# Two rings of split weight blocks as one tile each, with the stationary blocks 64 bytes in

## The chip, the cores and the metric

The kernel runs on one core of a Trainium2 chip. The metric is the device time of one execution in microseconds; the time before is the median of three executions.

## The reference

The kernel computes two layers on 256 tokens of width 1024. Each layer is a mixer (layer 0: latent attention with a low-rank query and key/value path; layer 1: attention over keys that an indexer selects), a layer norm, a PEER mixer (product keys choose 128 experts of 16,384 for each token), and a second layer norm.

```python
for i in range(DEPTH):
    if i % N_MIXERS == 0:
        m = _mla_mixer(x, ...)
    else:
        m = _dsa_mixer(x, ...)
    x = _layernorm(DN_ALPHA * x + m, ln_gain[i, 0], ln_bias[i, 0])
    f = _peer(x, peer_w_q[i], peer_sub_keys[i], peer_w_down[i], peer_w_up[i])
    x = _layernorm(DN_ALPHA * x + f, ln_gain[i, 1], ln_bias[i, 1])
...
# in _peer, for each block of tokens
u = w_down[e_blk]
a = jnp.einsum('td,ted->te', x_blk, u).astype(jnp.float32)
hg = (jax.nn.gelu(a, approximate=False) * g_blk).astype(w_up.dtype)
return jnp.einsum('te,ted->td', hg, w_up[e_blk]).astype(x_blk.dtype)
```

## The kernel before

**Split products.** Each float32 factor is split into a high part, rounded to the matmul's fp32r format, and a low part, the remainder. A product is three matmuls: high x high, high x low, low x high (`mm3`, `proj`, `rows`). The activations, transposed, live in two tiles `xh` and `xl` of 128 partitions x 8 x 256 values.

**PEER without a gather.** The kernel multiplies by all experts. In the down stage (tile `d`) each of 128 blocks of `w_down` gives the activations of 128 experts for 256 tokens; one-hot matmuls (tile `G`) place the gates, which multiply the gelu of `d`; the up stage (tile `y`) multiplies the result by 128 blocks of `w_up` into four PSUM banks. The two stages stand in each of two layers.

**The stream of weights.** `Stream` (line 51) carries every weight matrix as a row of blocks of 128 x 1024 values, in the order of the `ws.add` lines. A block is loaded by a DMA on SP's queue into one of four `raw` buffers (`_load`), cast by ScalarE into a `hi` buffer (L96), and subtracted by VectorE into a `lo` buffer (L100), or by GpSimd (L98) where `pooled` or `share` says so. `get()` hands out the next block and issues the cast and the subtraction of the block three further on (`AHEAD`), and the load of one three beyond that. `open()` and `close()` do the same in parts at the ends of the stages (`finish`), in an order written out there.

`his` and `los` are pools of four buffers of 4,096 bytes in each partition, used in turn; a buffer is overwritten when the last instruction that read it is done.

**Two uses of a block.** In `proj` and in the `up` helper of the latent attention the block is the weights: a slice of 128 columns is loaded into TensorE, and 256 columns of `xh`, `xl` (or of `V` and `U` in the groups `qn` and `qr`) stream past. So it is with mla_h (groups `h`, `krope`), mla_qk (`qn`, `qr`, `kn`), blocks 4 on of peer_q (`pq`), down (`d`), dsa_iq (`qi`), dsa_ik (`ki`, whose slices have 72 columns) and dsa_qk (`q`). In `rows` and in the lead units of `finish` the block is the moving operand, 512 columns at a time, and slices of `xh` and `xl` are the weights: mla_v and dsa_v (`v`), mla_w_o, dsa_w_o and up (`y`), blocks 0 to 3 of peer_q (`qw`).

**Where the operands stand.** In the built program `xh`, `xl`, the `raw`, `hi` and `lo` buffers and the arena begin at multiples of 512 bytes in their partitions. `V` and `U` (`oh_tile`, also used for `hot` and `gate`) lie behind the small tiles and begin at 64 bytes past a multiple of 128.

**What sets the order.** The tile framework orders the instructions of each engine by a simulated timeline at compile time, and draws the waits from the bytes that instructions touch. In the sparse attention part of the order is written out: `link` puts TensorE's matmuls and, from the first key projection on, VectorE's instructions (`dve`, which is also `ws.dve` there) in program order. In that part the steps of `attention` with `late` follow one another so: key projections of heads 4 and 5 (`meanwhile(4)`, whose two `get()` calls issue the cast and the subtraction of the last dsa_qk block and of the first dsa_w_o block), rotary copies and products of those heads (L507 to L516), scores of heads 2 and 3, their softmax (L547 to L559), then key projections of heads 6 and 7, outputs `o` of heads 0 and 1, and scores `s` of heads 4 and 5.

Of the kernel before, what the change touches and what calls it, by code (L numbers as in the profile page):

```python
# [11 lines left out]
F32R = mybir.dt.float32r  # L12
# [6 lines left out]
P = 128  # L19
T = 256  # L20
D = 1024
NC = D // P
# [21 lines left out]
FIRST = 4  # L44
WARM = 9
EARLY = 11264
GSCALE = 2.0 ** 14
DSA_POOL = 3
MAGIC = 12582912.0


class Stream:
# [5 lines left out]
    def __init__(self, nc, raw, hi, lo):  # L58
        self.nc, self.raw, self.hi, self.lo = nc, raw, hi, lo
        self.dve = self.act = lambda emit: emit()  # L60
        self.blocks, self.ready = [], []
        self.n_loaded = self.n_split = self.n_taken = 0
        self.tiles = []
        self.early = {}
        self.share = 0

    def add(self, src, w=D):
        self.blocks += [(src[i], w) for i in range(src.shape[0])]

    def _load(self, upto):  # L70
        while self.n_loaded <= min(upto, len(self.blocks) - 1):
            src, w = self.blocks[self.n_loaded]
            if self.n_loaded in self.early:
                t = self.early[self.n_loaded]
            else:
                t = self.raw.tile([P, D], F32, tag="raw", name=f"raw{self.n_loaded}")
                self.last = self.nc.sync.dma_start(t[:, :w], src).ins
            self.tiles.append(t)
            self.n_loaded += 1
# [8 lines left out]
    def _split(self, upto, pooled=False):  # L88
        nc = self.nc
        while self.n_split <= min(upto, len(self.blocks) - 1):  # L90
            w = self.blocks[self.n_split][1]
            self._load(self.n_split)
            raw = self.tiles[self.n_split][:, :w]
            hi = self.hi.tile([P, D], F32R, tag="hi", name=f"hi{self.n_split}")[:, :w]
            lo = self.lo.tile([P, D], F32R, tag="lo", name=f"lo{self.n_split}")[:, :w]
            self.act(lambda: nc.scalar.copy(hi, raw))  # L96
            if pooled or self.share and self.n_split % self.share == 0:
                nc.gpsimd.tensor_tensor(lo, raw, hi.bitcast(F32), op=ALU.subtract)  # L98
            else:
                self.dve(lambda: nc.vector.tensor_tensor(lo, raw, hi.bitcast(F32), op=ALU.subtract))  # L100
            self.ready.append((hi, lo))
            self.n_split += 1
# [7 lines left out]
    def open(self, queue):  # L110

        i = self.n_split
        assert i == self.n_taken
        self._load(i)
        raw = self.tiles[i]
        hi = self.hi.tile([P, D], F32R, tag="hi", name=f"hi{i}")
        lo = self.lo.tile([P, D], F32R, tag="lo", name=f"lo{i}")
        queue("act", lambda: self.nc.scalar.copy(hi, raw))
        self.ready.append((hi, lo))
        self.n_split += 1  # L120
        self.n_taken += 1
        return i
# [39 lines left out]
def tile_trunk(ctx: ExitStack, tc: tile.TileContext, ins, out: bass.AP):  # L162
    nc = tc.nc
    def pool(name, bufs, **kw):
        return ctx.enter_context(tc.tile_pool(name=name, bufs=bufs, **kw))
# [1 line left out]
    lead = pool("lead", 1)  # L167
    wide = pool("wide", 1)
    raws = pool("raws", 4)
    his = pool("his", 4)  # L170
    los = pool("los", 4)
    big = pool("big", 1)
    const = pool("const", 1)
    dram = pool("dram", 1, space=bass.MemoryType.DRAM)
# [35 lines left out]
    nc.vector.memset(ones, 1.0)  # L210
    nc.vector.memset(mhalf, -0.5)

    ws = Stream(nc, raws, his, los)
    ws.add(ins["mla_h"][0:6])
    ws.add(ins["mla_qk"])
    ws.add(ins["mla_v"])
    ws.add(ins["mla_w_o"])
    ws.add(ins["peer_q"][0])
    ws.add(ins["down"][0])
    ws.add(ins["up"][0])  # L220
    ws.add(ins["dsa_v"][0:FIRST])
    ws.add(ins["dsa_iq"])
    ws.add(ins["dsa_ik"], 576)
    ws.add(ins["dsa_v"][FIRST:NC])
    ws.add(ins["dsa_qk"])
    ws.add(ins["dsa_w_o"])
    ws.add(ins["peer_q"][1])
    ws.add(ins["down"][1])
    ws.add(ins["up"][1])

    chains = {}

# [574 lines left out]
    def dsa():  # L807
# [82 lines left out]
        for t in range(2):  # L890
            for n in range(2):
                nc.scalar.copy(v[:, t, n * 512 : (n + 1) * 512], v4[t][n])
        ws.share = DSA_POOL
        for h in range(0, HEADS, 2):
# [22 lines left out]
    def peer(li):  # L917
# [77 lines left out]
        def choose():  # L995
# [40 lines left out]
            gt, i1 = tail[:, 0:T], tail[:, T : 2 * T]  # L1036
            nc.vector.tensor_scalar(gt, pg[:, :T], GSCALE, None, op0=ALU.mult)
            nc.vector.tensor_copy(gate16, gt)
# [23 lines left out]
        def place(g4, done):  # L1062
# [8 lines left out]
            if done < P:  # L1071
                nc.scalar.mul(A[:, done:, tsl], pv[:, done:, :], 1.0 / GSCALE)
            if done:
                nc.vector.scalar_tensor_tensor(A[:, :done, tsl], pv[:, :done, :], 1.0 / GSCALE, A[:, :done, tsl],
                                               op0=ALU.mult, op1=ALU.mult)
# [54 lines left out]
    xt = Arena(arena, 30720).take(NC, T)  # L1130
    piece = [slice(c, c + 2) for c in range(0, NC, 2)]
    raw0 = raws.tile([P, D], F32, tag="raw", name="raw0")
    hi0 = his.tile([P, D], F32R, tag="hi", name="hi0")
    lo0 = los.tile([P, D], F32R, tag="lo", name="lo0")
    nc.sync.dma_start(raw0, ins["mla_h"][0])
    for c in range(0, NC, 4):
        last = nc.sync.dma_start(xt[:, c : c + 4, :], ins["xT"][c // 4])
    ws.blocks = ws.blocks[1:]
    with tc.issue_after(last.ins):
        ws._load(2)  # L1140

    def first(o):

# [129 lines left out]
```

## Time and profile before

| | |
|---|---|
| median of 3 executions | 1838.15 us (1837.89 to 1838.22) |
| profiled execution, span | 1836.6 us |
| TensorE busy | 1824.8 us, 99% |
| VectorE busy | 1317.8 us, 72% |
| ScalarE busy | 1056.2 us, 58% |
| GpSimd busy | 362.8 us, 20% |
| read from HBM | 329.16 MB, 182 GB/s over the span |

The profile is of one execution. A row of a timeline begins with the start and the length in microseconds, then the engine (PE is TensorE, DVE VectorE, ACT ScalarE, POOL GpSimd), the line in the kernel, the operation, and the tile written, with the tiles read behind the arrow; for a matmul the first of these is the moving operand or the weights as the program names them. "x12" is a count, and square brackets hold idle time before and what ended it. Lines L253 and L256 are helpers that issue every matmul and transpose, so groups of matmuls are told apart by their tiles. Matmuls are pipelined: each is shown longer than the distance between two starts, and the distance is what a run of them costs. A row of groups has the count, then busy time and mean ns of one, then the idle time before them.

### The profile page before, as it was taken

What the parts mean: (1) busy time and instruction counts of PE and PEld (TensorE: products, weight loads), DVE (VectorE), ACT (ScalarE), POOL (GpSimd) and SP (SyncE); (2) the same over time, 40 slices, a digit from 0 to 9 for tenths busy, and PEclk for the clock granted to TensorE, in tenths of its full rate; (3) what the DMA queues carried; (4) which work ended last, traced back from release to release, by engine and by line L of the source; (5) the groups of instructions that cost most, each with busy time, mean ns of one, the idle gap of its engine ahead of it and who ended that gap; (6) DMA issues with size and microseconds to landing.
All of it is one profiled execution on the core that took longest, in us unless ns stands there. A gap on an engine that the chain in (4) does not pass through costs nothing.

```text
span 1836.6 us, 32394 instructions
## 1 busy us (share of the span) xinstructions
PE 1824.8 (99%) x12495; PEld 1671.9 (91%) x12495; DVE 1317.8 (72%) x2348; ACT 1056.2 (58%) x1834; POOL 362.8 (20%) x265
## 2 busy tenths in 40 slices
PE   9999999999999999999999999999999999999998
PEld 8899999999998888888889899999999988888886
DVE  6689986788865555555688789957888765555555
ACT  6655456887764444444466555548877654444443
POOL 2002442445510000000022004504455300000000
PEclk9999999999999999999999999999999999999999
DMA  7554555444456555555646445554444475555553
GB/s 240 195 179 167 184 184 172 162 161 152 161 174 237 192 192 194 193 194 195 210 157 227 164 165 182 173 193 161 154 157 155 168 235 192 194 193 194 195 195 116
DMA packets 93468, 335.47 MB, mean 183 GB/s; under 512 B 10368, under 2 KB 11392, under 8 KB 93312
## 3 DMA queue, kind: packets, MB, share of 16 engines
q1 hardware_dynamic: 93024, 332.87, 52.9%
q8 instruction: 98, 1.61, 0.4%
q14 instruction: 58, 0.48, 0.1%
q10 hardware_dynamic: 288, 0.52, 0.1%
HBM read 329.16 MB, written 4.19 MB: 182 GB/s over the span
## 4 chain that ended last, share of the span: by engine, by line
PE 98%; DVE 1%; issue 1%; ACT 0%; DMA 0%; SPq 0%; DVEq 0%; POOLq 0%; POOL 0%; ACTq 0%
PE d L253 40%; PE y L253 40%; PE pq L253 4%; PE G L253 3%; PE q L253 3%; PE v L253 1%; PE qw L253 1%; PE s L253 1%; PE ps L253 1%; PE h L253 1%; PE qi L253 1%; PE o L253 1%; PE qn L253 0%; DMA arena<-in_xT 0%; PE kn L253 0%
## 5 line engine op out<-in xcount | busy, mean ns | idle before, releaser
L100 DVE TENSOR_TENSOR lo<-raw,hi 128x1024 fp32r<-128x1024 f32 (+1 forms) x579 | 763.9, 1321 | 345.0 <-ACT hi L96 344.1
L96 ACT CAST hi<-raw 128x1024 fp32r<-128x1024 f32 (+1 forms) x583 | 611.0, 1049 | 561.7 <-PE d L253 265.3
L253 PE MATMUL d<-xh,hi 128*128 128x256 f32 x2048 | 585.1, 286 | 0.0
L253 PE MATMUL d<-xh,lo 128*128 128x256 f32 x2048 | 579.2, 283 | 0.0
L253 PE MATMUL d<-xl,hi 128*128 128x256 f32 x2048 | 579.2, 283 | 0.0
L253 PEld LDWEIGHTS d<-xl,hi 128*128 128x128 f32 x2048 | 392.7, 192 | 0.0
L253 PEld LDWEIGHTS d<-xh,lo 128*128 128x128 f32 x2048 | 392.6, 192 | 0.0
L253 PEld LDWEIGHTS d<-xh,hi 128*128 128x128 f32 x2048 | 392.5, 192 | 0.0
L253 PE MATMUL y<-lo,xh 128*128 128x512 f32 x1088 | 337.7, 389 | 0.0
L253 PE MATMUL y<-hi,xh 128*128 128x512 f32 x1088 | 337.7, 390 | 0.0
L253 PE MATMUL y<-hi,xl 128*128 128x512 f32 x1088 | 337.3, 389 | 0.0
L1055 POOL TENSOR_TENSOR gate<-hot,gate 128x512 f16<-128x512 f16 x128 | 221.8, 1751 | 310.6 <-DVE hot L1053 310.6
L253 PEld LDWEIGHTS y<-lo,xh 128*128 128x128 f32 x1088 | 204.2, 188 | 42.7 <-DVE lo L100 0.3
L253 PEld LDWEIGHTS y<-hi,xl 128*128 128x128 f32 x1088 | 204.2, 188 | 42.4
L253 PEld LDWEIGHTS y<-hi,xh 128*128 128x128 f32 x1088 | 203.8, 188 | 41.8
L347 POOL TENSOR_TENSOR st<-st,mhalf 128x1 f32<-128x1 f32 x8 | 4.4, 551 | 827.2 <-DVE st L345 827.2
L1059 ACT ACTIVATE gate<-hot,rest 128x128 f16<-128x128 f16 x512 | 166.1, 413 | 0.9 <-DVE hot L1053 0.9
L1114 ACT CAST xh<-arena 128x512 fp32r<-128x512 f32 x128 | 79.8, 623 | 145.6 <-PE y L253 145.4
L1115 DVE TENSOR_TENSOR xl<-arena,xh 128x512 fp32r<-128x512 f32 x128 | 88.2, 692 | 73.5 <-ACT xh L1114 73.5
L1053 DVE TENSOR_TENSOR hot<-iota,place 128x1024 f16<-128x1024 f16 x128 | 84.9, 703 | 49.1 <-PE G L253 49.0
L1024 POOL TENSOR_TENSOR arena<-arena 128x800 f32<-128x800 f16 x32 | 78.8, 2482 | 38.8 <-DVE arena L1022 38.0
L253 PE MATMUL G<-gate,hot 128*128 128x128 f16 x1024 | 70.1, 221 | 0.0
(222 smaller groups left out, 1739.5 us busy)
## 6 DMA issues: line engine op xcount, KB each, us to landing
raw<-in_down SPq DMA_DIRECT2D x256, 512.0 KB, 3.2
raw<-in_up SPq DMA_DIRECT2D x256, 512.0 KB, 4.3
raw<-in_peer_q SPq DMA_DIRECT2D x24, 512.0 KB, 4.4
raw<-in_dsa_qk SPq DMA_DIRECT2D x16, 512.0 KB, 3.2
raw<-in_mla_w_o SPq DMA_DIRECT2D x8, 512.0 KB, 5.9
arena<-in_peer_q SPq DMA_DIRECT2D x8, 512.0 KB, 4.3
raw<-in_dsa_v SPq DMA_DIRECT2D x8, 512.0 KB, 4.3
raw<-in_dsa_w_o SPq DMA_DIRECT2D x8, 512.0 KB, 3.7
```

What stands on the lines that cost most here:

```text
L96: self.act(lambda: nc.scalar.copy(hi, raw))
L100: self.dve(lambda: nc.vector.tensor_tensor(lo, raw, hi.bitcast(F32), op=ALU.subtract))
L253: return pe(lambda: nc.tensor.matmul(o, l, r, start=start, stop=stop, skip_group_check=True))
L347: nc.gpsimd.tensor_tensor(st[:, 5:6], st[:, 4:5], mhalf, op=ALU.pow)
L1024: nc.gpsimd.tensor_tensor(o.rearrange("p k c -> p c k"), same, cell[t][:, h, :, None].to_broadcast([P, CELLS, TOPK]), op=ALU.mult)
L1053: nc.vector.tensor_tensor(hot, iota4[:, None].to_broadcast([P, 2, P, 4]), place16[:, :, None, four].to_broadcast([P, 2, P, 4]), op=ALU.is_ ...
L1055: nc.gpsimd.tensor_tensor(gate[:, 0], hot[:, 1].rearrange("p c j -> p j c"), gate16[:, four, None].to_broadcast([P, 4, P]), op=ALU.mult)
L1059: nc.scalar.mul(gate[:, 1, j, :], hot[:, 1, :, j], rest[:, t : t + 1])
L1114: nc.scalar.copy(hh, a)
L1115: nc.vector.tensor_tensor(al, a, hh.bitcast(F32), op=ALU.subtract)
```

## The change

The four `hi` buffers become one tile `hi` of 4 x 1024 + 64 values, the four `lo` buffers one tile `lo` of the same size. Block i stands at place i mod 4. A block added with `moving=True` begins at the start of its place; any other begins `SKEW` = 16 values, 64 bytes, further on, and so ends 64 bytes into the next place. The matrix peer_q is added in two parts, since its first four blocks are moving operands and the others weights. The first block, which was handled outside the stream, is now counted as block 0; `share` and the first `_load` are shifted by one to fit.

```diff
+RING = 4
+SKEW = 16
...
-    def add(self, src, w=D):
+    def add(self, src, w=D, moving=False):
         self.blocks += [(src[i], w) for i in range(src.shape[0])]
+        self.moving += [moving] * src.shape[0]
+
+    def parts(self, i):
+
+        skew = 0 if self.moving[i] else SKEW
+        at = i % RING * D + skew
+        return [ring[:, at : at + self.blocks[i][1]] for ring in (self.hi, self.lo)]
...
-            hi = self.hi.tile([P, D], F32R, tag="hi", name=f"hi{self.n_split}")[:, :w]
-            lo = self.lo.tile([P, D], F32R, tag="lo", name=f"lo{self.n_split}")[:, :w]
+            hi, lo = self.parts(self.n_split)
             self.act(lambda: nc.scalar.copy(hi, raw))
-            if pooled or self.share and self.n_split % self.share == 0:
+            if pooled or self.share and (self.n_split - 1) % self.share == 0:
...
-        hi = self.hi.tile([P, D], F32R, tag="hi", name=f"hi{i}")
-        lo = self.lo.tile([P, D], F32R, tag="lo", name=f"lo{i}")
+        hi, lo = self.parts(i)
...
-    his = pool("his", 4)
-    los = pool("los", 4)
+    rings = pool("rings", 1)
...
-    ws = Stream(nc, raws, his, los)
+    ring = [rings.tile([P, RING * D + 64], F32R, tag=k, name=k) for k in ("hi", "lo")]
+    ws = Stream(nc, raws, *ring)
     ws.add(ins["mla_h"][0:6])
     ws.add(ins["mla_qk"])
-    ws.add(ins["mla_v"])
-    ws.add(ins["mla_w_o"])
-    ws.add(ins["peer_q"][0])
+    ws.add(ins["mla_v"], moving=True)
+    ws.add(ins["mla_w_o"], moving=True)
+    ws.add(ins["peer_q"][0][0:FIRST], moving=True)
+    ws.add(ins["peer_q"][0][FIRST:])
     ws.add(ins["down"][0])
-    ws.add(ins["up"][0])
-    ws.add(ins["dsa_v"][0:FIRST])
+    ws.add(ins["up"][0], moving=True)
+    ws.add(ins["dsa_v"][0:FIRST], moving=True)
     ws.add(ins["dsa_iq"])
     ws.add(ins["dsa_ik"], 576)
-    ws.add(ins["dsa_v"][FIRST:NC])
+    ws.add(ins["dsa_v"][FIRST:NC], moving=True)
     ws.add(ins["dsa_qk"])
-    ws.add(ins["dsa_w_o"])
-    ws.add(ins["peer_q"][1])
+    ws.add(ins["dsa_w_o"], moving=True)
+    ws.add(ins["peer_q"][1][0:FIRST], moving=True)
+    ws.add(ins["peer_q"][1][FIRST:])
     ws.add(ins["down"][1])
-    ws.add(ins["up"][1])
+    ws.add(ins["up"][1], moving=True)
...
-    hi0 = his.tile([P, D], F32R, tag="hi", name="hi0")
-    lo0 = los.tile([P, D], F32R, tag="lo", name="lo0")
...
-    ws.blocks = ws.blocks[1:]
+    hi0, lo0 = ws.parts(0)
+    ws.n_loaded = ws.n_split = ws.n_taken = 1
+    ws.tiles.append(raw0)
+    ws.ready.append((hi0, lo0))
     with tc.issue_after(last.ins):
-        ws._load(2)
+        ws._load(3)
```

More of the change, by code (lines that the diff above doesn't have):

```diff
@@ L61, in __init__ @@
         self.blocks, self.ready = [], []
+        self.moving = []
         self.n_loaded = self.n_split = self.n_taken = 0
```

## The prediction

> **What bounds the kernel now.** I read the page first, then the groups kept apart by shape, the chain in order of time, and the timeline of the stretches in which the alignment of the operands differs.
>
> ```profile
> span 1836.6 us, 32394 instructions
> PE 1824.8 (99%) x12495; PEld 1671.9 (91%) x12495; DVE 1317.8 (72%) x2348; ACT 1056.2 (58%) x1834; POOL 362.8 (20%) x265
> PEclk9999999999999999999999999999999999999999
> PE d L253 40%; PE y L253 40%; PE pq L253 4%; PE G L253 3%; PE q L253 3%; PE v L253 1%; PE qw L253 1%; PE s L253 1%; PE ps L253 1%; PE h L253 1%; PE qi L253 1%; PE o L253 1%; PE qn L253 0%; DMA arena<-in_xT 0%; PE kn L253 0%
> ```
>
> TensorE is busy all the time at full granted clock, and the chain is its own queue. Only two things can move the end: how far apart matmuls start, and new waits of TensorE. The first is read from runs of matmuls in the chain (start, length, count), the counts from the groups:
>
> ```profile
> 23.22 2.88 PE krope L253 x24
> 43.13 3.83 PE kn L253 x32
> 151.56 146.63 PE d L253 x1222
> 548.60 348.19 PE y L253 x1536
> ...
> L253 PE MATMUL d<-xh,hi 128*128 128x256 f32 x2048 | 585.1, 286 | 0.0
> L253 PE MATMUL pq<-xh,hi 128*128 128x256 f32 x192 | 54.8, 285 | 0.0
> L253 PE MATMUL q<-xh,hi 128*128 128x256 f32 x128 | 36.9, 288 | 0.0
> L253 PE MATMUL h<-xh,hi 128*128 128x256 f32 x40 | 10.6, 303 | 0.2 <-ACT xh L1154 0.2
> L253 PE MATMUL qi<-xh,hi 128*128 128x256 f32 x32 | 9.1, 283 | 0.0
> L253 PE MATMUL kn<-xh,hi 128*128 128x256 f32 x16 | 4.6, 287 | 0.0
> L253 PE MATMUL krope<-xh,hi 128*128 128x256 f32 x8 | 2.3, 283 | 0.0
> ```
>
> A d matmul starts every 146.63/1222 = 120.0 ns, krope every 120.0, kn every 119.7; a y matmul, with twice the columns, every 348.19/1536 = 226.7. One column is (226.7 - 120.0)/256 = 0.417 ns, so either kind pays about 13.3 ns beside its columns, as much as 32 columns.
>
> In all of these both operands begin at multiples of 128 bytes: xh, xl and the ring's buffers stand at multiples of 512 in their partitions, and every slice begins at a further multiple of 512. One group is different. The moving operands V and U of qn and qr lie behind the small tiles, at 64 bytes past a multiple of 128, while their weights are ring blocks at a multiple of 512:
>
> ```profile
> 26.98 0.28 PE L253 MATMUL qn<-V,hi 128*128 128x256 f32 x1
> 29.93 0.28 PE L253 MATMUL qn<-V,lo 128*128 128x256 f32 x1
> ...
> 31.08 0.28 PE L253 MATMUL qn<-V,lo 128*128 128x256 f32 x1
> 34.48 0.28 PE L253 MATMUL qn<-V,lo 128*128 128x256 f32 x1
> ...
> 35.28 0.28 PE L253 MATMUL qr<-V,lo 128*128 128x256 f32 x1
> 39.16 0.28 PE L253 MATMUL qr<-V,lo 128*128 128x256 f32 x1
> ```
>
> From 26.98 to 29.93 qn starts 26 times more: 113.5 ns apart. From 31.08 to 34.48, after a short break, it starts 30 times more: 113.3. From 35.28 to 39.16 qr starts 33 times more: 117.6 ns. Same instruction, same columns, same clock, yet 6.5 and 2.4 ns less than krope just before and kn just after. My reading: loading the next weights while columns stream costs a fixed part (113.5 - 106.7 = 6.8 ns) and, when both streams step through memory in the same phase of 128 bytes, a collision of 6.5 ns, about 16 columns or 64 bytes. Half a period of offset avoids it, wholly in qn and partly in qr, which settled into another rhythm after its restart.
>
> **Part by part.** *The offset of weight blocks.* It gives d, pq, q, h, qi, kn and krope the relation of qn mirrored: weights at 64, moving xh and xl at 0. Each group above stands for three of the same count (hi with xh, hi with xl, lo with xh): 3 x (2048 + 192 + 128 + 40 + 32 + 16 + 8) = 7392 matmuls. At qn's rate that is 7392 x 6.5 ns = 48.0 us less; at qr's, 7392 x 2.4 = 17.7 us. I take qn's, since its rate was reached from two different starts, directly after krope and after the break, and qr's from one. The 24 ki matmuls have 72-column weights that begin at all multiples of 32 bytes already: nothing. The 72 qn and 36 qr matmuls lose what they have, as weights and V are then both at 64: 72 x 6.5 + 36 x 2.4 = 0.55 us more.
>
> *Moving blocks at 0.* y, v, qw and their weights in xh and xl keep the relation they have: nothing.
>
> *One tile for each ring.* The same four places, and a cast still waits for the last reader of the bytes that it overwrites. The cost lies at the seams. A weight block reaches 64 bytes into the next place. Where a moving block follows a weight block, its first 64 bytes are the last 64 of its predecessor, so its cast, issued three blocks ahead, must wait until the predecessor's matmuls end. That is so at down to up, twice, and dsa_qk to dsa_w_o. At mla_qk to mla_v the shared bytes are padding that no matmul reads, and the 576-wide dsa_ik ends short of the next place: nothing.
>
> ```profile
> 548.32 0.28 PE L253 MATMUL d<-xh,lo 128*128 128x256 f32 x1
> 548.44 0.63 PE L253 MATMUL y<-hi,xh 128*128 128x512 f32 x2
> 548.91 0.62 PE L253 MATMUL y<-lo,xh 128*128 128x512 f32 x2
> ...
> L100 DVE TENSOR_TENSOR lo<-raw,hi 128x1024 fp32r<-128x1024 f32 x578 | 763.2, 1322 | 345.0 <-ACT hi L96 344.1 <-PE qn L253 0.3
> L96 ACT CAST hi<-raw 128x1024 fp32r<-128x1024 f32 x582 | 610.4, 1050 | 561.7 <-PE d L253 265.3 <-PE y L253 209.1 <-PE pq L253 41.6
> ```
>
> Down to up: the last d ends at 548.60; cast until 549.65; y then starts 1.2 us late; two matmuls (0.47) cover part of the subtraction (1.32), another 0.8 us. 2.0 us each, 4.0 for both; between 2.4 (other matmuls with hi go first) and 6 (ACT does other casts first).
>
> The seam to dsa_w_o is worse, for there VectorE's order is written out: the subtraction of w_o's first block stands ahead of the rotary and softmax steps of heads 2 to 5.
>
> ```profile
> 983.89 2.36 DVE L100 TENSOR_TENSOR lo<-raw,hi 128x1024 fp32r<-128x1024 f32 x2
> 986.43 0.69 DVE L512 TENSOR_TENSOR arena<-q,arena 128x512 f32<-128x512 f32 x1 [0.18 <-ACT arena L508]
> 989.81 0.69 DVE L516 TENSOR_TENSOR arena<-arena 128x512 f32<-128x512 f32 x1 [1.58 <-POOL arena L509]
> 991.73 1.47 PE L253 MATMUL o<-arena 128*128 128x256 f32 x8
> 993.04 1.48 PE L253 MATMUL s<-arena 128*128 128x128 f32 x8
> ```
>
> The second of the two subtractions at 983.89 is that one. It will wait for the cast, and the cast for the last key projection, which ends when o begins at 991.73. Behind it on VectorE stand L512 to L516: from 986.43 to 990.50, less 1.58 of waiting, 2.5 us of work whose result the scores s of head 4 need. So s can start at 991.73 + 1.05 + 1.32 + 2.5 = 996.6 instead of 993.04: 3.6 us of TensorE idle. No deadlock: TensorE's own order needs none of that work before 993. Upper bound, the whole delay of the subtraction: 991.73 + 1.05 + 1.32 - 986.25 = 7.9 us. The normalisations behind it arrive a little later still; I take 4.0, near the lower end, since later y matmuls need only what is on time.
>
> *Weights after moving blocks* (dsa_v to dsa_iq and to dsa_qk, peer_q twice): the first weight cast now waits for the reader of two places, one block more.
>
> ```profile
> 906.70 1.06 ACT L96 CAST hi<-raw 128x1024 fp32r<-128x1024 f32 x1 [3.32 <-DMA raw<-in_dsa_iq]
> 906.62 1.75 PE L253 MATMUL v<-lo,xh 128*128 128x512 f32 x7
> 908.66 0.28 PE L253 MATMUL qi<-xh,hi 128*128 128x256 f32 x1
> ```
>
> Here there are 0.9 us between the cast's end and its first use. Of the seven v matmuls the last four belong to the block after the one waited for, so that one ends three matmuls (3 x 0.227) and a drain of some 0.15 after 906.62, about 0.7 us after the old start of the cast. Nothing each; 0.5 us each if that slack is gone.
>
> *What comes due next.* With d 5% faster, VectorE's selection work could become late:
>
> ```profile
> sum 80.00, PE 80.00 PEld 80.00 DVE 78.61 ACT 41.38 POOL 42.66; mean PE 20.00 PEld 20.00 DVE 19.65 ACT 10.35 POOL 10.66
> ```
>
> That is 167 to 247 us: VectorE works 78.6 of 80, and TensorE would want the stretch in 75.7. The three blocks prepared ahead (8 us) cover the 2.9: nothing, at most 3 us in each of two layers.
>
> Renumbering the blocks (index 0 now counted, share shifted by one) issues the same loads in the same order: nothing, either way.
>
> Sum: -48.0 + 0.55 + 4.0 + 4.0 = -39.5 us. The profiled span of 1836.6 becomes 1797.1; it stands 1.55 below the median 1838.15, so the median becomes 1798.7, say **1799**.
>
> **The rivals.** *The worse rhythm.* If everything settles as qr did, the sum is -17.7 + 8.6 = -9.1: 1829. Against it stands only that qn did better twice. Between lies a split: 1222 of a layer's 3072 d matmuls stand in one unbroken run; the rest are broken by G groups, after which each run begins anew. If those 2 x 1850 go at 117.6, 15.2 us of the gain is gone: 1814.
>
> *The offset does nothing, and the seams decide.* Then qn's rate has another cause, such as which operands alternate, and d stays at 120.0. The time is 1838.15 + 8 = 1846 (1842 to 1853): slower. It decides wherever the gain per matmul is under 8.0 us / 7392 = 1.1 ns. For it: qn and qr have the same offset and differ by 4.1 ns, so offset is not all. Against it: krope and kn, on either side, have the same form and clock and take 120. The Trainium skill (TensorE: Matmul & The Clock Gate, in its account of a matmul's life under DRAIN) says that TensorE has two independent read ports on SBUF, one for the moving operand and one for weights. By that rule relative addresses should not matter and this rival holds; 113.5 beside 120.0 speaks against it.
>
> *The straddle costs.* In qn the moving operand stands across the 128-byte boundaries, here the weights do; if that costs a collision more instead of one less, the time is 1838 + 48 + 8 = 1894. No row shows it.
>
> **How the numbers follow.** qn's rhythm (1793 to 1804, by the bounds of the seams) 0.45; the split 0.15; qr's 0.14; offset without effect 0.20; straddle 0.06. The range takes the first three and part of the fourth: 1793 to 1845. A change under 0.2% (3.7 us) can't be told from none. Faster 0.74; same 0.06 (from the fourth case, with a gain that about pays for the seams); slower 0.20.
>
> **What would show it.** Right: long d runs start every 113 to 114 ns, y stays at 226.7, qn and qr go to 120; TensorE idles some 2 us at the start of both y stages and about 4 us before the scores of head 4, with VectorE waiting in L100 behind the cast. Wrong: d at 120.0 (offset without effect), d at 117 to 118 (rhythm), different rates before and after the first G group (split), y changed (lo's place relative to hi's, now 16,640 bytes instead of 16,384, matters), or seams of many microseconds.

## The result, and the profile after

The changed kernel takes 1812.95 us (median of 4 runs, 1810.23 to 1814.72) against 1838.18 (4 runs, 1837.89 to 1838.52): a ratio of 0.986, 95% interval 0.985 to 0.988. It is faster by 1.4%, inside the range and 14 us above the forecast of 1799. The profiled execution has a time of 1814.72 us and a span of 1812.9.

In this kernel the shared bytes change a part of what is computed. The last block of the first layer's down has the last 16 of its 1,024 columns overwritten by the first up block, whose cast is issued three blocks earlier, and the first 16 columns of three dsa_v blocks are those of dsa_qk blocks. Its time is that of the same number of matmuls.

First the page, then the chain (start, length, group, count) of the kernel after.

```profile
span 1812.9 us, 32388 instructions
PE 1794.7 (99%) x12495; PEld 1640.2 (90%) x12495; DVE 1317.3 (73%) x2348; ACT 1056.3 (58%) x1834; POOL 363.1 (20%) x265
PE 90%; DVE 8%; issue 1%; DMA 0%; ACT 0%; SPq 0%; DVEq 0%; POOLq 0%; POOL 0%; ACTq 0%
```

```profile
21.93 2.72 PE krope L263 x24
...
144.67 2.96 PE d L263 x26
148.52 35.16 PE d L263 x310
...
252.30 39.62 PE d L263 x334
292.36 11.31 PE d L263 x96
...
304.59 5.71 PE d L263 x48
311.22 5.51 PE d L263 x48
317.66 5.53 PE d L263 x48
534.19 348.19 PE y L263 x1536
1067.97 2.96 PE d L263 x26
1457.30 342.31 PE y L263 x1510
```

TensorE is still 99% busy, but 8% of the chain is now VectorE. krope starts every 113.3 ns (2.72/24) and y every 226.7, as forecast. d has two rates: 113.4 in the run at 148.52 and 118.6 in the run at 252.30, and between the G groups two runs of 48 in three are quick (5.51, 5.53) and one slow (5.71). From the start times of its matmuls, blocks 0 to 18 go at 113.3 ns, 19 to 51 at 117.8, and those behind them, whose runs the G groups break, at a mixture of the two; no run of d goes at 120.0.

The same rows of the kernel before that the prediction did not show:

```profile
147.56 3.11 PE d L253 x26
298.63 11.51 PE d L253 x96
1079.91 3.11 PE d L253 x26
1480.94 342.31 PE y L253 x1510
```

Differences of these starts share out the 23.7 us. Before the first d: 147.56 - 144.67 = 2.9 gained. First down stage: (548.60 - 147.56) - (534.19 - 144.67) = 11.5 gained, 3.4 of it up to the run of 96 (298.63 and 292.36) and 8.1 behind it. First up stage and the sparse attention: 531.3 before, 533.8 after, 2.5 lost. Second down stage: 11.7 gained. The rest: 0.1.

The waits of TensorE in the kernel after (sum, times, longest) and the stretch in which the new ones lie:

```profile
PE v L263 <- ACT hi L105: 2.7, 3, 1.2
PE d L263 <- DVE lo L109: 2.2, 2, 1.1
PE v L263 <- DVE lo L109: 2.1, 3, 0.8
```

```profile
913.85 0.73 PE L263 MATMUL v<-hi,xh 128*128 128x512 f32 x2 [1.18 <-ACT hi L105]
915.37 0.73 PE L263 MATMUL v<-lo,xh 128*128 128x512 f32 x2 [0.78 <-DVE lo L109]
```

None of these three groups waits in the kernel before. The seams cost where the prediction had put nothing (*weights after moving blocks*): at dsa_v, 4.8 us. At the three places where it had put 8 us, y follows d, and s follows o, without a wait.

### The profile page after: what moved, and what is told of

Read it like the earlier page. It is cut to its first block, busy times and chain, and to the rows that moved or that the text cites. A ratio compares the mean times of both kernels' runs of the same rounds, so it can differ in the third digit from the quotient of the medians.

```text
span 1812.9 us, 32388 instructions
## 1 busy us (share of the span) xinstructions
PE 1794.7 (99%) x12495; PEld 1640.2 (90%) x12495; DVE 1317.3 (73%) x2348; ACT 1056.3 (58%) x1834; POOL 363.1 (20%) x265
## 4 chain that ended last, share of the span: by engine, by line
PE 90%; DVE 8%; issue 1%; DMA 0%; ACT 0%; SPq 0%; DVEq 0%; POOLq 0%; POOL 0%; ACTq 0%
PE y L263 41%; PE d L263 32%; PE pq L263 4%; PE G L263 3%; DVE lo L109 3%; PE q L263 3%; PE v L263 1%; DVE arena L1038 1%; PE qw L263 1%; PE s L263 1%; PE ps L263 1%; DVE arena L1032 1%; PE h L263 1%; PE qi L263 1%; DVE arena L992 1%
## 5 line engine op out<-in xcount | busy, mean ns | idle before, releaser
L263 PE MATMUL d<-xh,hi 128*128 128x256 f32 x2048 | 576.7, 282 | 0.0
L263 PE MATMUL d<-xh,lo 128*128 128x256 f32 x2048 | 570.5, 279 | 2.2 <-DVE lo L109 2.2
L263 PE MATMUL d<-xl,hi 128*128 128x256 f32 x2048 | 570.4, 279 | 0.0
L263 PEld LDWEIGHTS d<-xh,lo 128*128 128x128 f32 x2048 | 386.8, 189 | 2.6 <-DVE lo L109 2.6
L263 PEld LDWEIGHTS d<-xl,hi 128*128 128x128 f32 x2048 | 385.6, 188 | 0.0
L263 PEld LDWEIGHTS d<-xh,hi 128*128 128x128 f32 x2048 | 385.3, 188 | 0.0
```

The lines of the kernel that those rows point to most:

```text
L263: return pe(lambda: nc.tensor.matmul(o, l, r, start=start, stop=stop, skip_group_check=True))
```

## Experiments

The theory after the trace: a matmul's rate depends on where the weights stand relative to the moving operand; a run of d settles in one of two rhythms; the seams cost waits of v; and VectorE's selection bounds blocks 19 to 52. Rivals: the ring's one tile made the gain, not the offset; or the weights' own alignment counts, not the relation of the two streams. e1, e2, e5, e9 and e12 were timed once, the others four times.

**e1: the ring without the offset.**

```diff
-SKEW = 16
+SKEW = 0
```

> The one-tile rings alone, with every block at 0 bytes past a multiple of 128 (SKEW = 0). T1 (the offset between the two operand streams makes the gain): d, kn and krope return to 120.0 ns between starts, long d runs of one rhythm, no wait of v for a cast or subtraction; span about 1837, time about 1838. T2 (the rings' one tile and its changed schedule make the gain, the offset none): d stays at 113 to 118 and the time at about 1813. T1 gives qn and qr their 113.5 and 117.6 back.

1837.96 us. krope and d are back at 120.0, and no v waits:

```profile
22.66 2.88 PE krope L263 x24
...
151.04 146.63 PE d L263 x1222
```

The one tile gains nothing. The offset makes the gain.

**e2: 128 bytes instead of 64.**

```diff
-SKEW = 16
+SKEW = 32
```

> Weight blocks stand 128 bytes in (SKEW = 32); moving blocks at 0. With the wider shift the first 32 columns of some v and y blocks share bytes with a neighbour, so those values of the computation are altered. T1 (a period of 128 bytes): the streams are in phase again, d at 120.0 and the time 1838 plus the waits of v at the seams (about 5), so 1838 to 1845. Rival (any offset helps, or the period is longer than 128): d at 113 to 118 and the time at about 1813.

1841.29 us, beside 1838.29 for the kernel before: the time that a period of 128 would give. The long run is at 120.0, but the runs between G groups took 5.75 us, less than the 5.80 of e1.

```profile
151.95 146.64 PE d L263 x1222
...
311.33 5.75 PE d L263 x48
```

So 128 bytes are nearly, not wholly, the same as 0: a first sign that the period is longer. The waits of v are those of the kernel after, 2.7 and 2.1 us.

**e3: places of 1,040 values, so that no byte is shared** (offsets modulo 128 kept by alternating the skew).

```diff
-        skew = 0 if self.moving[i] else SKEW
-        at = i % RING * D + skew
+        place = i % RING
+        skew = SKEW if self.moving[i] == (place % 2 == 1) else 0
+        at = place * (D + SKEW) + skew
```

> The same offsets modulo 128 (weights at 64, moving blocks at 0) but places of 1040 values, so that no block shares a byte with its neighbour. If the seams cost what the waits of v for the cast and the subtraction at the sparse attention's dsa_v add up to in the kernel after (4.8 us), and the rhythms stay as they are: 1808. If those waits hid other work: 1812 to 1814. The rhythm of d (113.3 or 117.75) can turn out otherwise in a run that starts differently, worth at most 6144 x 4.4 ns = 27 us either way around 1813; by T1 each run of d is at one of these two values and never at 120.

1822.59 us, ratio 0.992 (0.990 to 0.993): a miss. The waits of v are gone, but y went from 226.7 to 353.51/1536 = 230.2 ns:

```profile
150.39 35.16 PE d L264 x310
254.25 38.15 PE d L264 x334
292.83 11.32 PE d L264 x96
...
536.89 353.51 PE y L264 x1536
```

By its start times, y runs at 226.7 ns in the two places where moving blocks stand at 0 modulo 256, and at 233.3 in the two where they stand at 128: 128 is not the period. In d the run at 254.25 is at 114.2, quicker than after, yet TensorE waited in front of it:

```profile
PE d L264 <- DVE lo L110: 3.6, 3, 1.7
```

**e4: every block 64 bytes in, the moving ones too.**

```diff
-        skew = 0 if self.moving[i] else SKEW
-        at = i % RING * D + skew
+        at = i % RING * D + SKEW
```

> Every block stands 64 bytes in, the moving ones too; no seams. T1 (only the offset between the two streams counts): y, v and qw leave 226.7 ns and go to about 220.0 (226.7 less 6.7), or to some 224 in the slower rhythm; d stays at 113 to 118. 3072 y matmuls save 3072 x 6.7 = 20.6 us at the most, 7 in the slower rhythm, and the seams 4.8: 1787 to 1802. T3 (the weights' own alignment counts, not the offset between the streams): y stays at 226.7, time about 1808.

1817.05 us, ratio 0.989 (0.987 to 0.990). Both expectations for y failed: it neither stayed nor became quicker, but rose to 351.57/1536 = 228.9 ns.

```profile
149.76 35.16 PE d L262 x310
...
292.18 10.90 PE d L262 x96
533.60 351.57 PE y L262 x1536
```

y changed although its weights, in xh and xl, stayed where they were. That rules out the weights' own alignment for y. The moving operand's own alignment is still possible here; e5 settles that, and whether y has another best offset than d.

**e5: the price by itself.** The core of the edit, a row of matmuls at given offsets in an otherwise empty kernel:

```diff
+    for i, k in enumerate(letters):
+        gap(3)
+        d("dw" + k, 8 * i, 0)
+        gap(5)
+        d("dw" + k, 8 * i, 0)
```

> The disputed price by itself: this kernel leaves the whole computation out (its output is a copy of x) and runs rows of matmuls in the forms of d (three matmuls for each 128-column slice of weights, 256 columns) and of y (512 columns), with nothing else on the core. Names give form and offset: dw a to p, weights at 0, 32, 64 ... 480 bytes past a multiple of 512 with the moving operand at 0; dm a to p, the moving operand so with the weights at 0; ym and yw the same for the form of y; rx and ry a to h, the form of d with weights at 64 after 1 to 8 short matmuls (ry with the low weights 256 bytes further). T1 (offset between the two streams, period 128 bytes): dw and dm both repeat every fourth letter, 120.0 at a, e, i, m and 113.3 or 117.75 at c, g, k, o; y 226.7 at a, e, i, m and 228.9 at c, g, k, o; rx and ry hold both 113.3 and 117.75. Rival (period 256): the letters e and m differ from a and i: about 118.6 for d, 233.3 for y. Rival (weights' own alignment alone): dm stays at 120.0 for all letters.

1106 us. Rows of 72 matmuls (d) and 36 (y), from the chain; the first letters are the form and the operand that is shifted (dw: d with shifted weights, dm: d with the shifted moving operand, ym: y with the shifted moving operand), the last one the shift in steps of 32 bytes (a is 0, c 64, e 128, g 192). In rx the weights stand at 64 and the letter counts the short matmuls ahead of the row:

```profile
18.88 8.68 PE dwa L51 x72
...
54.34 8.24 PE dwc L51 x72
...
88.77 8.70 PE dwe L51 x72
...
124.39 8.53 PE dwg L51 x72
...
159.41 8.68 PE dwi L51 x72
...
335.18 8.54 PE dmc L51 x72
...
405.83 8.23 PE dmg L51 x72
...
580.84 8.24 PE yma L51 x36
...
615.20 8.31 PE ymc L51 x36
...
684.59 8.44 PE ymg L51 x36
...
1006.58 5.54 PE rxc L51 x48
...
1012.26 5.73 PE rxd L51 x48
...
1086.64 8.62 PE both L51 x72
```

With the weights at 64 (dwc) a row takes 8.24 us, with the moving operand at 64 (dmc) 8.54, with it at 192 (dmg) 8.23: what counts is weights minus moving operand, and in these rows 64 is not the same as -64. Shifting both by 64 ("both") gives d back at 120.0, so neither operand's own alignment decides. Letters i to p repeat a to h: the period is 256 bytes, the rival's. Over the second half of each row, ns from start to start:

| weights minus moving, modulo 256 | 0 | 32 | 64 | 96 | 128 | 160 | 192 | 224 |
|---|---|---|---|---|---|---|---|---|
| d (256 columns) | 120.0 | 118.4 | 113.3 | 117.4 | 118.7 or 120.0 | 120.0 | 117.8 | 116.7 or 117.8 |
| y (512 columns) | 226.7 | 233.3 | 233.3 | 234.4 | 232.0 to 232.7 | 233.3 | 228.9 or 233.3 | 233.3 |

Shifts were tried in steps of 32 bytes. Where two rates stand, the same row began in another phase, after other short matmuls; y at 128 had 233.3 in e3. At 64 seven of eight starts gave 113.3 (rxc) and one 117.8 (rxd). The low weights' extra 256 bytes (ry) change nothing.

**e6: no shared byte, and right modulo 256.**

```diff
-SKEW = 16
+PLACE = (16, 1040, 2128, 3152), (0, 1088, 2112, 3200)
...
-        skew = 0 if self.moving[i] else SKEW
-        at = i % RING * D + skew
+        at = PLACE[self.moving[i]][i % RING]
```

> The kernel after with places that share no byte, moving blocks at 0 and weight blocks at 64 bytes past a multiple of 256 (the iota tile moves into the arena to make room). By the runs so far the offset between the streams counts modulo 256: y goes back to 226.7 (from 230.2 with the places of e3_seamless), d is at 113.3 or 117.75, v no longer waits for a cast or a subtraction: the kernel after less the 4.8 us of those waits, 1808, with the rhythm of d as an unknown of up to 10 us either way. If the waits of v hid something that waits anyway, 1813.

1813.14 us, ratio 0.987 (0.985 to 0.988): as the kernel after.

```profile
149.80 143.93 PE d L262 x1222
294.16 11.31 PE d L262 x96
...
536.00 348.19 PE y L262 x1536
```

y is at 226.7 and v waits for nothing: from the first ki to the first q, 17.9 us instead of 23.5 in the kernel after (17.9 before). But d began in the slow rhythm and kept it, 143.93/1222 = 117.8 ns, in both layers, and the peer queries too; blocks 0 to 18 alone took 2.0 us more in each layer. So the seams cost 5.6 us, and a start in the other rhythm took the saving back.

**e7 and e8: one selection step for each block of d**, in e6 and in the kernel after.

```diff
-STEPS = (1, 1, 1, 2)
+STEPS = (1, 1, 1, 1)
```

> As e6_noshare, and one step of the selection for each block of d instead of five for four, so that VectorE's selection work spreads over 65 blocks instead of 52. If VectorE's selection sets the pace of blocks 19 to 52 (its busy time there is 67.97 of 68.00 us in the kernel after): no wait of d for a subtraction, d at 113.3 through those blocks, 33 blocks x 24 x 4.4 ns + 1.1 us = 4.6 us less in each of two layers, and the G groups, three to a pair of blocks, leave more d in long runs: e6 less 5 to 12 us. If not (the switch of rhythm at block 19 has another cause): e6 within 2 us.

> The kernel after with that change of steps alone (the shared bytes remain, and with them the altered first 16 columns at the seams). VectorE's pace as the cause: 5 to 12 us less than 1813, no wait of d for a subtraction, the five waits of v unchanged. Otherwise within 2 us of 1813.

1822.48 us (ratio 0.992, 0.990 to 0.993) and 1821.94 (the same): misses, 9 us slower than e6 and the kernel after. The edit did not spread the selection; VectorE stayed full in e7:

```profile
180.00:253.00 73.00, 73.00 (x622) 73.00 (x622) 72.26 (x209) 37.91 (x43) 42.12 (x32) 1.00 0.55 181
```

(us, busy PE, PEld, DVE, ACT, POOL, granted clock.) What it did move are the G groups: by the trace of the first layer, in 83 breaks of d instead of 34, and blocks 52 to 127 took 247.0 us (e7) instead of 241.9 (e6). So the times of e7 and e8 do not test VectorE's pace. The blocks ahead of the G groups tell a little of it: in e8 d went at 113.3 in most of blocks 19 to 51, where the kernel after had 117.8, but waited up to 1.7 us for a subtraction at blocks 34 to 38. They took 93.3 us instead of 95.0; at 113.3 throughout it would be 792 x 0.1133 = 89.8. e8 shows something else, at the waits of v:

```profile
912.00:918.00 6.00, 4.06 (x18) 2.77 (x17) 4.75 (x7) 4.02 (x7) 1.29 (x1) 0.98 0.58 196
918.00:924.00 6.00, 5.71 (x16) 3.50 (x16) 0.19 (x2) 1.35 (x2) 0.00 (x0) 0.50 0.26 88
```

After waits of 1.18 and 0.76 us the granted clock fell to 0.50, and ki to q took 26.9 us.

**e9: 192 bytes.**

```diff
-SKEW = 16
+SKEW = 48
```

> Weight blocks 192 bytes in instead of 64 (the overhang alters the first 48 columns at the seams). By the table of e5_micro (only the offset of the weights against the moving operand counts, modulo 256, and 192 is another case than 64): d at 117.8 throughout and never at 113.3, y at 226.7; 7392 matmuls save 2.2 ns each, 16 us, less the waits of v, 4.8: about 1827. If 64 and 192 were the same (a period of 128): d a mixture of 113.3 and 117.75, time about 1813.

1830.33 us, 3 more than expected. As the table says, d is at 117.8 throughout and never at 113.3:

```profile
151.31 143.93 PE d L263 x1222
```

Only the queries q of the sparse attention had 113.3 in 258 of their 372 gaps: the quicker state exists at 192 too, though no row of e5 and no d of e9 found it.

**e10 to e12: every sixth subtraction to GpSimd during the selection**, in the kernel after, in e6 and in the kernel before.

```diff
         for b0 in range(0, NKEYS, 2):
+            ws.share = 0 if ready else 6
```

> The kernel after, with every sixth subtraction of the weight stream given to GpSimd while the selection runs (VectorE 1.3 us less each, about 9 of them in blocks 0 to 52; GpSimd takes 2.7 us for one). If VectorE sets the pace of blocks 19 to 52: those blocks go from 95.0 us to between 89.8 (792 x 113.33) and 93.3 (792 x 117.78), the wait of d for a subtraction goes, and if its lateness is what switched the rhythm at block 19, d stays at 113.3 there: 2 x 5 us less, about 1803. If VectorE is not the cause: 95.0 as before, 1813.

> e6_noshare with the same relief of VectorE. There d ran at 117.8 through all of blocks 1 to 52, without any wait (93.6 us for blocks 19 to 52). If d starts in that rhythm again: no gain, 1813. If it starts at 113.3 and VectorE was the limit: 2 us less in blocks 0 to 18 and 3.8 in 19 to 52, in each of two layers, about 1801.

> The kernel before with the same relief of VectorE and nothing else: d is at 120.0 and waits for nothing there, so no gain: 1838 within 1. If it gains, the relief has an effect of its own and e10 does not tell of the offset.

1824.61 (ratio 0.993, 0.991 to 0.995), 1822.00 (0.991, 0.989 to 0.993) and 1849.16 us. These are misses: all three lost 9 to 12 us, the kernel before too, so e10 does not test the offset. In e10:

```profile
PE d L263 <- DVE lo L109: 7.1, 5, 2.2
PE d L263 <- POOL lo L107: 4.5, 4, 1.1
```

```profile
198.00:204.00 6.00, 4.54 (x38) 4.15 (x36) 6.00 (x9) 1.90 (x4) 3.91 (x2) 1.00 0.42 148
```

TensorE works 4.54 of 6 us while VectorE is full: the time freed there was filled with selection work from further on (from the first d to block 34 of the first layer, VectorE did 84.0 us of work other than subtractions, in the kernel after 75.5), and subtractions came late on both engines. No version tried here beats the kernel after.

## Why the prediction was right, and where it was not

*The cause.* Right, and now shown: e1 takes the offset away and the gain goes; e5 has the price without the rest. The reading behind it was right in kind (an extra of about 16 columns that depends on how the two streams stand to each other) and wrong in its period, 256 bytes and not 128. Nor is it a collision in phase for both forms: in phase d has its worst rate, 120.0, and y its best, 226.7. Why the offset counts so stays open. The forecast still read the right row of the table, by luck. V, at 220,352 bytes, is at 192 modulo 256, so qn with weights at 0 stood at -192, which is 64, and a weight block at 64 with xh at 0 stands at 64 too. Had V stood at 64 modulo 256, qn would have stood at 192, the row at which d ran at 117.8 ns in e9, and the same argument would have carried the price of that row over to weights at 64.

*The rival that the offset does nothing* has fallen. The Trainium skill's statement behind it (TensorE: Matmul & The Clock Gate, Part 2: What happens when you issue a matmul; two independent read ports, so that loading weights takes nothing from the running matmul) does not describe these rows: at one clock and one shape, 113.3 to 120.0 ns by relative address alone.

*The step that failed: 7392 matmuls at 6.5 ns, 48.0 us.* By the start times (gaps between d matmuls, without the breaks) d fell from 119.9 to 115.6 ns on average, 4.3 and not 6.5; 6,144 of them make 26 us instead of 40, and pq, q, h, qi, kn and krope bring some 6 more. What the prediction called qr's worse rhythm is a second steady state of the same offset: 117.8. Which of the two a run takes depends on the phase of its start (e5), and a late matmul within the run can switch it: in the kernel after, d changed in block 19, right behind a matmul that started 132 ns after the one ahead of it (127 in the second layer), without a wait that the profile lists. It need not: in e8 a matmul of the same block came after 170 ns, and d stayed at 113.3; and the waits of 1.1 us in the kernel after, at block 38, did not bring 113.3 back. The forecast gave this 0.15 as "the split", at 1814, because of the breaks at the G groups. The time agrees, the reason only half: two thirds of those runs were quick, and the long run, which the split had left quick, was slow from block 19 on.

*What comes due next.* Put at nothing, at most 3 us in each layer. From the start of d's long run to the run of 96 behind the first G groups' preparation the kernel before took 298.63 - 151.56 = 147.1 us, after 292.36 - 148.52 = 143.8, e6 144.4 without a wait, e3 and e4 142.4 with d at 113.3 and waits for VectorE's subtraction. At 113.3 throughout it would be 1222 x 0.1133 and 0.4 of other matmuls: 138.9. Blocks 19 to 51 of e8 miss the same 3.5 us. So the chain's 8% of VectorE is real, and 3.5 us in each layer cannot be had from TensorE alone: slightly beyond the bound given. That taking work off VectorE would free them is not shown, since VectorE stayed full in e7, e8, e10 and e11.

*The seams.* 8 us at three places became 5.6 at another. Two errors. Down to the second up, and dsa_qk to dsa_w_o, pass from place 3 to place 0, where the overhang falls into the padding; the prediction did not follow i mod 4. And it took the cast as the one that waits. The order of dependences is that of the program: a cast issued three blocks ahead stands before the read of the block whose bytes it shares, so the reader waits for the writer and reads its data, where the prediction had the writer wait for the reader. That is down to the first up, where it costs no time, and dsa_v, where each of three blocks waits for the cast and the subtraction of the block three further on.

*As forecast:* y at 226.7; qn and qr slower, to 119.3 and 118.6 (offset 128 in the table); nothing from the renumbering.

*The sum by what was measured:* about 32 us of matmul rate, less 5.6 at the seams, 2.2 of d's waits and 0.4 in qn and qr, is 24; the spans differ by 23.7.

## What to carry to other kernels

Where TensorE's queue is the whole chain, compare the start-to-start time of equal matmuls whose operands stand at different addresses: here, with fp32r operands and a weight load for each matmul, a shift of 64 bytes is worth 5.6%, and the best shift is another for 256 columns (64) than for 512 (0). Take the offset of the two operands to each other, modulo 256, from the built program, and measure it in rows of their own before rebuilding buffers around it. When buffers become slices of one tile, no block may reach into another's bytes, and a quicker stage has to be held against the engine that prepares its data.

## What the runs showed of the hardware

- One offset can have two steady rates (113.3 and 117.8 ns at 64), and a run can keep the one it fell into for 1,222 matmuls (e6). Whether the spread of the kernel after (4.5 us over four runs, 0.6 before) comes from that was not tried.
- Equal shapes had rates of 113.3 to 120.0 and 226.7 to 234.4 ns; 512 columns are best in phase, where 256 have their worst rate.
- The granted clock can give way after waits of little more than a microsecond, and need not. In e8 TensorE was busy for 4.06 of 6 us and then had 0.50 of its clock; e2 and e9 show 0.72 in six microseconds at the same place. The kernel after has such waits too (TensorE busy for 2.04 us from 912 to 916) and kept 1.00 there, as did e6, which has none. The Trainium skill (TensorE: Matmul & The Clock Gate, Part 1: The HAM clock gate) ties the drop to an idle window of about 3.4 us; no single wait here was that long.
